# A hybrid SSD and MLP layer: first MLP product by seven quarter products, its result through DRAM, second product by token halves

## The chip, the core and the metric

The kernel runs on one core of a Trainium2 chip. The metric is device time in microseconds (us) of one execution, the median of three runs. TensorE (PE) multiplies, VectorE (DVE), ScalarE (ACT) and GpSimd (POOL) do the rest, and SyncE (SP) issues nearly all transfers, in order: a transfer that waits holds up every transfer behind it.

## The reference

One layer on 1024 tokens of 1024 channels, in float32:

```
h = x*(1+sc1) + sh1                                  # sh, sc, g: from a conditioning vector
z, xbc, dt = split(h @ w_in);  xbc = silu(conv4(xbc))
y = ssd_scan(...) + d*xs                             # Mamba-2, chunks of 64 tokens, 8 groups
y = group_rmsnorm(y * silu(z)) * norm_w              # the "gate"
x = layer_norm(alpha*x + g1 * (y @ w_out))           # w_out: 2048 x 1024
h = x*(1+sc2) + sh2
x = layer_norm(alpha*x + g2 * (relu(h @ w1)**2 @ w2))   # w1: 1024 x 4096, w2: 4096 x 1024
```

## The kernel before

Each float32 product is three TensorE passes: every operand is split into a rounded part (`...h`, a cast by `high`, line 114) and the rest (`...l`, a subtraction by `low`, line 117), and hi*hi, lo*hi and hi*lo are accumulated in PSUM. A matmul here is 128x128 weights against 128x512 columns.

**Phase A** computes `w_in` (line 141), the convolution, and the SSD group by group, in chunks (`py`, lines 357 and 362; `y`, line 366). A finished half group passes the gate: POOL multiplies by `zt` (line 385), ACT squares (388, 389), DVE adds, splits, PE sums over channels with a matrix of ones (397, 398), DVE and ACT take the inverse root (400 to 407), DVE scales (409), and SP stores it to `y_dram` (411). The last group has four such gates.

**Phase B** multiplies by `w_out` in four passes, `out_pass(T, Dh)`: token half T, output half Dh, 192 matmuls (line 584) each. Each of 16 steps loads 128 rows of `w_out` (`owr`, 557) and, for Dh=0, of `y_dram` (`yr`, 560), splits them and feeds four PSUM banks. For T=0 the split `y` tiles lie in a pool of their own (`yp0`), for T=1 partly in the second token half of `h2h`/`h2l`. At the end of a pass DVE multiplies by `g1b` (593) and adds to the row in `res`. `ln1(T)` normalises, transposes (531) and splits into `h2h`/`h2l`; `residual(T)` turns `res` into the residual of the next layer norm.

**Phase C** goes over 32 tiles of 128 FF channels. `up(f)` is 48 matmuls (653), squared ReLU and a split into `uh`/`ul`; `load2(f)` loads 128 rows of `w2`, multiplies by `g2b` (635) and splits. After every two tiles `down` adds their product, 12 matmuls (684) per 128 tokens, to `res` (690). The last four tiles are taken together, and each 128 tokens are then normalised and stored (lines 694 to 717).

The order in each engine's queue is set by a scheduler when the program is built; buffers that share memory with others wait for the last use of those. `psm` and `ps2` are the two halves of PSUM, two tiles of two banks each.

Of the kernel before, what the change touches and what calls it, by code (L numbers as in the profile page):

```python
# [9 lines left out]
F32 = mybir.dt.float32  # L10
F32R = mybir.dt.float32r
AF = mybir.ActivationFunctionType
ALU = mybir.AluOpType
# [21 lines left out]
def trunk(ctx: ExitStack, tc: tile.TileContext, a: dict, out: bass.AP):  # L35
# [5 lines left out]
    a_dram = dram.tile([NC * NH, C], F32, name="a_dram")  # L41

    # ---------------------------------------------------------------- constants
# [37 lines left out]
    mod2 = const([P, 2, KT], "mod2")          # sh2, sc2 per channel  # L81
# [76 lines left out]
    # head: conditioning, h and the first three channel tiles, k outermost  # L158
# [59 lines left out]
    def head_mm(j, w, lo):  # L218
# [8 lines left out]
        for hf in range(2):  # L227
            # the columns beside the weights are zero: each half of the tokens has its own partitions
# [31 lines left out]
    # dt, its decays and their running sums  # L260
# [152 lines left out]
    # the remaining conditioning vectors, one block of 512 columns at a time  # L413
# [69 lines left out]
    # ---------------------------------------------------------------- phase B  # L483
    ps2 = ctx.enter_context(tc.tile_pool(name="ps2", bufs=2, space=PSUM, reuse_waits="tile"))
    per = ctx.enter_context(tc.tile_pool(name="per", bufs=1, side="right", reuse_waits="tile"))
# [20 lines left out]
    lbb = lnp.tile([P, D], F32, name="lbb", tag="lbb")  # L506
    ob = ExitStack()
    ob_pool = ob.enter_context(tc.tile_pool(name="ob", bufs=2, side="right", reuse_waits="tile"))
    yp0 = ExitStack()
# [6 lines left out]


    def ln1(T, sts):
# [4 lines left out]
        for t in range(4):  # L523
            row = res[:, T * 4 + t, :]
            vec.tensor_scalar(row, row, mv[:, t, 0:1], r[:, t:t + 1], op0=ALU.subtract, op1=ALU.mult)
        ts = slice(T * 512, T * 512 + 512)
        for k in range(KT):
            if k % 2 == 0:
                pt = ps2.tile([P, 2, 512], F32, name="mm2", tag="mm2")
# [265 lines left out]
```

## Time and profile before

| | us |
|---|---|
| time, median of 3 runs | 1698.74 (1698.41 to 1700.62) |
| span of the profiled execution | 1694.5 |
| PE busy | 1603.7 (95%) |
| DVE busy | 1117.5 (66%) |
| ACT, POOL busy | 606.2 (36%), 555.4 (33%) |

The span is what the profiler saw from the first to the last instruction; no other time of that execution is given. A busy share is a mean over phases that differ: what a phase is limited by is read from the waits inside it. PEclk is the clock granted to TensorE as a share of full speed.

### The profile page before, as it was taken

To read this page: it belongs to the slowest core of one execution; us is meant where nothing else is said; L and a number is where in the kernel's file an instruction comes from. 1 tells how busy PE (TensorE), PEld (TensorE's weight loads), DVE (VectorE), ACT (ScalarE), POOL (GpSimd) and SP (SyncE) were. 2 spreads that over 40 slices of the span, in tenths; PEclk is the share of its full clock that TensorE was granted. 3 is DMA by queue.
4 is the path that set the end of the run, shared out by engine and by line. 5 is a ranking of instruction groups with operands and counts; after the bars stand their busy time and mean duration, and the time that the engine had idled before them with its cause. 6 is when DMAs were issued, how large, how long until landed. Compare 5 with 4: busy or idle time off the path is not lost.

```text
span 1694.5 us, 19835 instructions
## 1 busy us (share of the span) xinstructions
PE 1603.7 (95%) x7768; PEld 1299.6 (77%) x7768; DVE 1117.5 (66%) x1676; ACT 606.2 (36%) x720; POOL 555.4 (33%) x282
## 2 busy tenths in 40 slices
PE   6998898999999999988999889999999999999996
PEld 5886677878787777766877668888888888888884
DVE  7759988788878778877468483444444444444458
ACT  3554364555554555644342222111111111111122
POOL 2323323242424232424555442222222222222225
PEclk9999999999999999999999989999999999999998
DMA  8324433233323121134762221111111111111102
GB/s 320 123 89 137 119 100 104 96 106 106 106 94 112 63 88 63 44 120 157 231 219 73 71 66 59 50 50 50 50 49 40 48 48 42 47 42 47 38 13 99
DMA packets 56973, 151.66 MB, mean 90 GB/s; under 512 B 7344, under 2 KB 8880, under 8 KB 55984
## 3 DMA queue, kind: packets, MB, share of 16 engines
q1 hardware_dynamic: 56592, 150.37, 27.1%
q8 instruction: 61, 1.00, 0.2%
q14 instruction: 32, 0.26, 0.1%
q10 hardware_dynamic: 288, 0.03, 0.0%
HBM read 137.66 MB, written 12.71 MB: 89 GB/s over the span
## 4 chain that ended last, share of the span: by engine, by line
PE 67%; DVE 21%; issue 4%; DMA 4%; ACT 3%; POOL 1%; SPq 0%; DVEq 0%; ACTq 0%; POOLq 0%
PE mm L653 20%; PE mm L684 19%; PE mm L141 17%; PE mm L584 6%; DVE dec L344 3%; DVE mac L424 2%; DMA adr<-in_ada_r_dram 1%; DVE macc L200 1%; PE py L357 1%; PE pst L370 1%; DVE dec L347 1%; DVE Bt L154 1%; DVE y L366 1%; DVE Ct L154 1%; DVE y L117 1%
## 5 line engine op out<-in xcount | busy, mean ns | idle before, releaser
L690 DVE TENSOR_TENSOR res<-res,mm 128x1024 f32<-128x1024 f32 x119 | 145.0, 1219 | 246.5 <-PE mm L684 246.4
L141 PE MATMUL mm<-hl,whi 128*128 128x512 f32 x720 | 286.7, 398 | 0.0
L141 PE MATMUL mm<-hh,whi 128*128 128x512 f32 x720 | 286.6, 398 | 0.0
L141 PE MATMUL mm<-hh,wlo 128*128 128x512 f32 x720 | 285.8, 397 | 0.0
L653 PE MATMUL mm<-h2h,w1l 128*128 128x512 f32 x512 | 200.3, 391 | 1.6 <-POOL w1l L117 1.6
L653 PE MATMUL mm<-h2h,w1h 128*128 128x512 f32 x512 | 200.7, 392 | 1.1 <-DVE h2h L114 1.1
L653 PE MATMUL mm<-h2l,w1h 128*128 128x512 f32 x512 | 199.6, 391 | 2.2 <-POOL h2l L117 2.2
L684 PE MATMUL mm<-w2h,uh 128*128 128x512 f32 x496 | 194.3, 392 | 6.5 <-DVE res L690 6.5
L684 PE MATMUL mm<-w2l,uh 128*128 128x512 f32 x496 | 193.7, 390 | 0.0
L684 PE MATMUL mm<-w2h,ul 128*128 128x512 f32 x496 | 193.7, 390 | 0.0
L117 POOL TENSOR_TENSOR w2l<-w2r,w2h 128x1024 fp32r<-128x1024 f32 x31 | 74.4, 2419 | 347.5 <-ACT w2h L114 347.5
L117 POOL TENSOR_TENSOR wlo<-wraw,whi 128x1024 fp32r<-128x1024 f32 x45 | 111.3, 2473 | 228.8 <-ACT whi L114 228.8
L114 ACT CAST w2h<-w2r 128x1024 fp32r<-128x1024 f32 x31 | 32.6, 1052 | 352.9 <-PE mm L684 349.6
L141 PEld LDWEIGHTS mm<-hh,wlo 128*128 128x128 f32 x720 | 136.0, 189 | 28.8 <-issue 1.7
L141 PEld LDWEIGHTS mm<-hh,whi 128*128 128x128 f32 x720 | 136.0, 189 | 28.4 <-issue 1.3
L141 PEld LDWEIGHTS mm<-hl,whi 128*128 128x128 f32 x720 | 136.0, 189 | 28.3 <-issue 1.4
L351 POOL TENSOR_TENSOR ea<-ea,Ct 128x512 f32<-128x512 f32 x56 | 79.6, 1421 | 207.0 <-ACT ea L350 181.1
L584 PE MATMUL mm<-owh,y 128*128 128x512 f32 x384 | 122.7, 400 | 9.5 <-ACT y L114 4.0
L117 POOL TENSOR_TENSOR w1l<-w1r,w1h 128x1024 fp32r<-128x1024 f32 x32 | 93.9, 2936 | 111.5 <-ACT w1h L114 111.5
L117 POOL TENSOR_TENSOR owl<-owr,owh 128x512 fp32r<-128x512 f32 x61 | 90.8, 1498 | 90.4 <-ACT owh L114 86.6
L684 PEld LDWEIGHTS mm<-w2h,uh 128*128 128x128 f32 x496 | 93.5, 189 | 27.5 <-DVE res L690 8.2
L653 PEld LDWEIGHTS mm<-h2l,w1h 128*128 128x128 f32 x512 | 96.3, 188 | 23.0 <-POOL h2l L117 2.8
(239 smaller groups left out, 2974.3 us busy)
## 6 DMA issues: line engine op xcount, KB each, us to landing
wraw<-in_w_in_dram SPq DMA_DIRECT2D x45, 512.0 KB, 4.3
adr<-in_ada_r_dram SPq DMA_DIRECT2D x32, 512.0 KB, 3.5
ar<-a_dram SPq DMA_DIRECT2D x64, 256.0 KB, 3.3
owr<-in_w_out_dram SPq DMA_DIRECT2D x64, 256.0 KB, 3.1
w1r<-in_w_dram SPq DMA_DIRECT2D x32, 512.0 KB, 3.5
w2r<-in_w_dram SPq DMA_DIRECT2D x32, 512.0 KB, 3.6
y_dram<-y SPq DMA_DIRECT2D x32, 256.0 KB, 2.1
yr<-y_dram SPq DMA_DIRECT2D x32, 256.0 KB, 3.1
```

Of the source, the lines that this page charges most:

```text
L114: return (act.copy if eng is act else eng.tensor_copy)(hi, src)
L117: eng.tensor_tensor(lo, src, hi.bitcast(F32), op=ALU.subtract)
L141: pe.matmul(ps[:, hf, :], lhsT=w_[:, k, :], rhs=x_[:, k, ts], start=(k == 0 and i == 0), stop=(k == KT - 1 and i == 2))
L154: vec.scalar_tensor_tensor(dst[:, j:S], src[:, 0:S - j], convw[:, ct, 3 - j:4 - j], dst[:, j:S], op0=ALU.mult, op1=ALU.add)
L200: vec.scalar_tensor_tensor(av_, ada[:, k, :], csil[:, k:k + 1], av_, op0=ALU.mult, op1=ALU.add)
L344: vec.tensor_scalar(dec[:, h, :], ar[:, h, :], acs[:, c, g * HPG + h:g * HPG + h + 1], 0.0, op0=ALU.subtract, op1=ALU.min)
L351: pool.tensor_tensor(ea, ea, G["C"][:, ts].unsqueeze(1).broadcast_to([P, HPG, C]), op=ALU.mult)
L424: vec.scalar_tensor_tensor(acc, ad[:, i, :], csil[:, k:k + 1], acc, op0=ALU.mult, op1=ALU.add)
L584: pe.matmul(po[t // 2][:, t % 2, :], lhsT=l_[:, sl], rhs=r_, start=(k_ == 0 and i == 0), stop=(k_ == 15 and i == 2))
L653: pe.matmul(ps[:, hf, :], lhsT=w_[:, k, :], rhs=x_[:, k, ts], start=(k == 0 and i == 0), stop=(k == KT - 1 and i == 2))
L684: pe.matmul(pos[Dh], lhsT=l_[:, sl], rhs=r_[:, ds_], start=(f == fs[0] and i == 0), stop=(f == fs[-1] and i == 2))
L690: vec.tensor_tensor(row, row, po.rearrange("p a b -> p (a b)"), op=ALU.add)
```

## The change

Four things are done. (1) For FF tiles 4 to 31, taken in 14 pairs, `h @ w1` for two FF tiles and all tokens is computed by Winograd's form of Strassen's scheme: the contraction is cut into halves, FF and tokens too, and seven quarter products of 12 matmuls take the place of eight. DVE forms sums of the weight quarters (`s1` to `s4`) for each pair, and of the input blocks (`t1` to `t4`) once. Tiles 0 to 3 are computed plainly. (2) The squared ReLU is stored to `u_dram`, and the residual rows to `x1_dram`; `res` is gone, its rows live in four buffers of `rowp`. (3) The second product comes after the first is complete, by token halves `down(T)`: eight PSUM banks hold 512 tokens by 1024 channels and accumulate over all 32 tiles; `w2` and `u` are loaded and split in each half, and `g2b` is multiplied in when the banks are emptied. (4) `h2h`/`h2l` become blocks `b11`, `b12`, `b21`, `b22` in the pool on the right, and the first eight split `y` tiles use `b12` and `b22` for both token halves; the pools on the left are laid out anew.

```diff
-    h2h = per.tile([P, KT, S], F32R, name="h2h", tag="h2h")
-    h2l = per.tile([P, KT, S], F32R, name="h2l", tag="h2l")
-    res = per.tile([P, NC, D], F32, name="res", tag="res")
+    def h2_block(nm):
+        return [per.tile([P, 4, 512], F32R, name=nm + q, tag=nm + q) for q in "hl"]
+    B = {(kh, T): h2_block(f"b{kh + 1}{T + 1}") for T in range(2) for kh in range(2)}
...
+    mpa = up_.enter_context(tc.tile_pool(name="mpa", bufs=2, reuse_waits="tile"))
+    rowp = up_.enter_context(tc.tile_pool(name="rowp", bufs=4, reuse_waits="tile"))
     ob_pool = ob.enter_context(tc.tile_pool(name="ob", bufs=2, side="right", reuse_waits="tile"))
-    yp0_pool = yp0.enter_context(tc.tile_pool(name="yp0", bufs=1, reuse_waits="tile"))
+    yp = ypx.enter_context(tc.tile_pool(name="yp", bufs=1, reuse_waits="tile"))
...
-        if T == 1 and k < KT:
-            return h2h[:, k, 512:1024], h2l[:, k, 512:1024]
+        if k < KT:
+            return [b_[:, k % 4, :] for b_ in B[k // 4, 1]]
...
+    def product(dst, w, x, first=False):
+        for k in range(4):
+            for i, (w_, x_) in enumerate(((w[0], x[0]), (w[1], x[0]), (w[0], x[1]))):
+                pe.matmul(dst, lhsT=w_[:, k, :], rhs=x_[:, k, :], start=(first and k == 0 and i == 0),
+                          stop=(k == 3 and i == 2), skip_group_check=not first)
...
+    def up_quad(p):
+        r0, r1 = load1(f0), load1(f1)
...
+        vec.tensor_tensor(s[2], a11, a21, op=ALU.subtract)
+        vec.tensor_tensor(s[0], a21, a22, op=ALU.add)
+        vec.tensor_tensor(s[1], s[0], a11, op=ALU.subtract)
+        vec.tensor_tensor(s[3], a12, s[1], op=ALU.subtract)
+        a1 = forms1(r0)
...
+        product(X, [w_[:, 0:4, :] for w_ in a1], X11, True)
+        product(Q, F["s3"], TF["t3"], True)
+        act.copy(Y, X)
+        product(Y, F["s2"], TF["t2"])
+        act.copy(q7, Q)
+        product(X, [w_[:, 4:8, :] for w_ in a1], X21)
+        act.copy(Z, Y)
+        act.activation(u0[:, 0:512], X, AF.Relu)
+        product(Y, F["s1"], TF["t1"])
+        vec.tensor_tensor(u1[:, 512:S], Y, q7, op=ALU.add)
+        product(Z, F["a22"], TF["t4"])
+        vec.tensor_tensor(u1[:, 0:512], Z, q7, op=ALU.add)
+        product(Y, F["s4"], X22)
+        vec.scalar_tensor_tensor(u1, u1, 0.0, u1, op0=ALU.max, op1=ALU.mult)
+        u_store(f1, u1)
+        act.activation(u0[:, 512:S], Y, AF.Relu)
+        pool.tensor_tensor(u0, u0, u0, op=ALU.mult)
+        u_store(f0, u0)
...
+    def load2(f, T):
         sp.dma_start(w2r, a["w2"][f])
+        sp.dma_start(ur, u_dram[f][:, T * 512:T * 512 + 512])
...
+        split(ur, uh, ul, act, vec)
+        split(w2r, w2h, w2l, act, vec if f % 2 == 0 else pool)
...
+    def down(T):
+        po = [(psm.tile([P, 2, 512], F32, name="mm", tag="mm") if t < 2 else
+               ps2.tile([P, 2, 512], F32, name="mm2", tag="mm2")) for t in range(4)]
...
+        KF = 4
+        for f in range(NF - KF):
+            ops = load2(f, T)
+            for t in range(4):
+                for Dh in range(2):
+                    mms(f, t, Dh, ops)
...
+            sp.dma_start(row, x1_dram[tt])
...
+                vec.tensor_tensor(tm[:, q], src[:, q], g2b[:, q], op=ALU.mult)
+                vec.tensor_tensor(row[:, q], row[:, q], tm[:, q], op=ALU.add)
```

How the queues change is shown at three places. First SP at the end of phase A, before; `y_dram12` and `y_dram13` are the stores of the first of the last four gates.

```order
L325 DMA ar_6279<-a_dram_73 128x512 [waits DMAHW3_49,DVE_49]
L557 DMA owr_6449<-in_w_out_dram 128x512 [waits DMAHW6_49,Pool_49]
L560 DMA yr_6451<-y_dram0_57 128x512 [waits DMAHW7_49]
L557 DMA owr_6474<-in_w_out_dram 128x512
L560 DMA yr_6476<-y_dram1_58 128x512
L557 DMA owr_6498<-in_w_out_dram 128x512
L557 DMA owr_6522<-in_w_out_dram 128x512 [waits DMAHW6_49,DVE_49]
L560 DMA yr_6500<-y_dram2_59 128x512 [waits DMAHW7_49,DMAHW4_49,DVE_49]
```

The same place in the changed kernel; `DMAHW...` is a wait for earlier transfers, here the four last stores of `y_dram`.

```order
L413 DMA y_dram12_69<-y_5147 128x512 [waits DVE_49]
L413 DMA y_dram13_70<-y_5147 128x512 [waits DMAHW4_49,DVE_49]
L413 DMA y_dram12_69<-y_5423 128x512 [waits DMAHW5_49,DVE_49]
L413 DMA y_dram13_70<-y_5423 128x512 [waits DVE_49]
L413 DMA y_dram14_71<-y_5812 128x512 [waits DVE_49]
L413 DMA y_dram15_72<-y_5812 128x512 [waits DMAHW0_49,DVE_49]
L413 DMA y_dram14_71<-y_6082 128x512 [waits DMAHW1_49,DVE_49]
L413 DMA y_dram15_72<-y_6082 128x512 [waits DMAHW2_49,DVE_49]
L571 DMA owr_6500<-in_w_out_dram 128x512 [waits DMAHW3_49,DMAHW4_49,DMAHW2_49,DMAHW1_49]
L574 DMA yr_6502<-y_dram0_57 128x512 [waits DMAHW7_49,DMAHW0_49]
```

The first loads of phase B stood ahead of the last gates' stores; now they stand behind all of them, and the first of them waits for the last stores, since its buffer takes over memory of the last gates.

Second, PE at the same time, before: the matrix of ones (`pr`) of a gate among the matmuls of the first pass.

```order
L584 MATMUL mm_6447<-owh_6647,y0_8_6650 128x512
L398 MATMUL pr_6375<-sl_6372,ones_r_91 128x512
L584 MATMUL mm_6447<-owl_6648,y0_8_6650 128x512
L584 MATMUL mm_6447<-owh_6647,y1_8_6651 128x512
L584 MATMUL mm_6447<-owh_6647,y0_8_6650 128x512
```

PE in the changed kernel, where the last gate's two `pr` matmuls and the first matmul of the first pass stand.

```order
L359 MATMUL py_6339<-dec_6329,X_6325 64x128 x2
L364 MATMUL py_6339<-ea_6336,hn_6260 64x128 x2
L359 MATMUL py_6339<-dec_6329,X_6325 64x128 x2
L364 MATMUL py_6339<-ea_6336,hn_6260 64x128 x2
L399 MATMUL pr_6442<-sh_6438,ones_r_131 128x512
L400 MATMUL pr_6442<-sl_6439,ones_r_131 128x512
L598 MATMUL mm_6498<-owh_6504,b12h_6474 128x512
L598 MATMUL mm_6499<-owh_6504,b12h_6474 128x512
```

No matmul of the first pass stands ahead of the last gate's any more.

Third, SP towards the end of phase C, before: weights of both products in turn.

```order
L612 DMA w1r_11660<-in_w1_dram 128x1024
L612 DMA w1r_11729<-in_w1_dram 128x1024
L634 DMA w2r_11666<-in_w2_dram 128x1024
L634 DMA w2r_11735<-in_w2_dram 128x1024
L612 DMA w1r_11798<-in_w1_dram 128x1024
L634 DMA w2r_11804<-in_w2_dram 128x1024
```

SP in the changed kernel, from the last pair of FF tiles to the second product; `xrow` are the residual rows.

```order
L665 DMA u_dram31_105<-row_10247 128x1024
L803 DMA xrow_11417<-x1_dram0_106 128x1024
L803 DMA xrow_11467<-x1_dram1_107 128x1024
L803 DMA xrow_11515<-x1_dram2_108 128x1024
L803 DMA xrow_11565<-x1_dram3_109 128x1024
L803 DMA xrow_12673<-x1_dram4_110 128x1024
L665 DMA u_dram30_104<-row_10246 128x1024
L771 DMA w2r_10361<-in_w2_dram 128x1024
L773 DMA ur_10363<-u_dram0_74 128x512
```

The first load of `w2` now stands behind the last store of the first product and behind five loads of residual rows, the second of which waits for the last matmuls of the first product.

## Rows read from the trace of the kernel before

**Rows 1.** The page's first part: busy time, share of the span, instructions of each engine.
```profile
PE 1603.7 (95%) x7768; PEld 1299.6 (77%) x7768; DVE 1117.5 (66%) x1676; ACT 606.2 (36%) x720; POOL 555.4 (33%) x282
```

**Rows 2.** Windows: stretch, length, busy time by engine, PEclk, DMA share, GB/s.
```profile
741.00:807.00 66.00, 54.04 (x245) 41.14 (x244) 49.74 (x71) 31.63 (x51) 28.18 (x17) 0.92 0.49 156
807.00:958.00 151.00, 144.45 (x634) 117.63 (x633) 85.18 (x104) 45.75 (x75) 80.26 (x53) 0.98 0.49 161
958.00:1012.00 54.00, 39.15 (x162) 29.46 (x161) 47.23 (x51) 16.63 (x25) 27.18 (x12) 0.87 0.15 49
1108.00:1632.00 524.00, 524.00 (x2313) 434.04 (x2312) 243.03 (x165) 97.66 (x96) 127.59 (x48) 1.00 0.14 45
```

**Rows 3.** Chain that ended last, towards the end: start, us, what.
```profile
1602.94 5.44 PE mm L684 x24
1608.38 23.80 PE mm L653 x105
1632.18 9.99 PE mm L684 x44
...
1680.36 4.46 PE mm L684 x12
1684.83 0.69 DVE res L687
```

**Rows 4.** Timeline of PE around the start of phase B: start, us, instruction, idle before.
```profile
741.50 0.40 PE L398 MATMUL pr<-sl,ones_r 128*128 128x512 f32 x1
745.23 1.19 PE L584 MATMUL mm<-owh,y 128*128 128x512 f32 x2 [3.34 <-ACT r L403]
...
800.45 0.80 PE L584 MATMUL mm<-owh,y 128*128 128x512 f32 x1 [3.96 <-ACT y L114]
801.04 0.63 PE L584 MATMUL mm<-owl,y 128*128 128x512 f32 x1
...
806.89 0.85 PE L584 MATMUL mm<-owh,y 128*128 128x512 f32 x3
```

**Rows 5.** Timeline of DVE: last step of two gates, and the first pass's end.
```profile
751.50 2.44 DVE L409 SCALAR_TENSOR_TENSOR y<-y,nwcol,r 128x512 f32<-128x512 f32 x2
...
805.64 1.42 DVE L409 SCALAR_TENSOR_TENSOR y<-y,nwcol,r 128x512 f32<-128x512 f32 x2
807.32 1.29 DVE L593 TENSOR_TENSOR tm<-mm,g1b 128x512 f32<-128x512 f32 x2 [0.26 <-PE mm L584]
```

**Rows 6.** Groups by line, 741 to 808 us: busy us, mean ns, idle before.
```profile
L385 POOL TENSOR_TENSOR y<-y,zt 128x1024 f32<-128x1024 f32 x2 | 4.7, 2370 | 9.9 <-ACT zt L444 6.9 <-DVE y L366 3.0
```

**Rows 7.** DMA issues: count, KB each, median us to landing.
```profile
owr<-in_w_out_dram SPq DMA_DIRECT2D x64, 256.0 KB, 3.1
w2r<-in_w_dram SPq DMA_DIRECT2D x32, 512.0 KB, 3.6
y_dram<-y SPq DMA_DIRECT2D x32, 256.0 KB, 2.1
```

**Rows 8.** What PE waited for from 740 us: us in total, times, longest.
```profile
PE mm L531 <- DVE res L525: 12.4, 3, 7.4
PE mm L684 <- DVE res L690: 6.5, 4, 4.6
```

**Rows 9.** Windows: the second pass of the output product.
```profile
815.00:855.00 40.00, 39.83 (x177) 32.65 (x176) 16.57 (x25) 13.10 (x23) 20.28 (x15) 1.00 0.74 245
```

**Rows 10.** Groups by line, 1100 to 1632 us: steady phase C.
```profile
L117 POOL TENSOR_TENSOR w1l<-w1r,w1h 128x1024 fp32r<-128x1024 f32 x24 | 70.8, 2952 | 85.6 <-ACT w1h L114 85.6
L114 ACT CAST w2h<-w2r 128x1024 fp32r<-128x1024 f32 x24 | 25.3, 1053 | 314.0 <-PE mm L684 314.0
```

**Rows 11.** Timeline of DVE in the last stage: evictions and normalisation.
```profile
1671.46 1.22 DVE L690 TENSOR_TENSOR res<-res,mm 128x1024 f32<-128x1024 f32 x1
...
1676.31 2.29 DVE L498 TENSOR_TENSOR rq<-rr 128x1 f32<-128x1 f32 x1
...
1679.09 1.22 DVE L690 TENSOR_TENSOR res<-res,mm 128x1024 f32<-128x1024 f32 x1
```

More of the change, by code (lines that the diff above doesn't have):

```diff
@@ L668, in down @@
-    def down(fs, toks, final=False):
-        for t in toks:
-            sl = slice(t * P, (t + 1) * P)
-            po = ps2.tile([P, 2, 512], F32, name="mm2", tag="mm2")
-            last = final and t == NC - 1
-            pos = [po[:, 0, :], (ps2.tile([P, 2, 512], F32, name="mm2", tag="mm2") if last else po)[:, 1, :]]
-            row = res[:, t, :]
-            steps = [(f, Dh) for f in fs for Dh in range(2)]
+    yt, sts = [], []
+    out_pass(1, 0, yt, sts)
+    ws1 = [forms1(load1(f)) for f in range(2)]
@@ new lines, in trunk, with up_plain @@
+    out_pass(1, 1, yt, sts)
+    ob.close()
+    ypx.close()
+    NS = 4
+    lt1 = ExitStack()
+    lt = lt1.enter_context(tc.tile_pool(name="lt", bufs=2, reuse_waits="tile"))
+    tst = ExitStack()
+    tpool = tst.enter_context(tc.tile_pool(name="tpool", bufs=1, side="right", reuse_waits="tile"))
+    h2q = {}
+    ups = {}
+    def up_plain(f, w, T):
+        if T == 0:
+            pl_, tg = (psm, "mm") if f % 4 < 2 else (ps2, "mm2")
+            ups[f] = pl_.tile([P, 2, 512], F32, name=tg, tag=tg)
+        for k in range(KT):
+            bh, bl = B[k // 4, T]
+            for i, (w_, x_) in enumerate(((w[0], bh), (w[1], bh), (w[0], bl))):
+                pe.matmul(ups[f][:, T, :], lhsT=w_[:, k, :], rhs=x_[:, k % 4, :],
+                          start=(k == 0 and i == 0), stop=(k == KT - 1 and i == 2))
@@ new lines, in u_store, with up_evict @@
+    def u_store(f, u, cols=slice(0, S)):
+        sp.dma_start(u_dram[f][:, cols], u[:, cols])
+    def up_evict(f):
+        u = rowp.tile([P, S], F32, name="row", tag="row")
+        act.activation(u, ups[f].rearrange("p a b -> p (a b)"), AF.Relu)
+        vec.tensor_tensor(u, u, u, op=ALU.mult)
+        u_store(f, u)
+    up_plain(0, ws1[0], 0)
+    up_plain(1, ws1[1], 0)
+    ln1(1, sts, lt, h2q)
+    up_plain(0, ws1[0], 1)
+    up_plain(1, ws1[1], 1)
+    residual(1)
+    ws2 = [forms1(load1(f)) for f in range(2, NS)]
@@ new lines, in trunk @@
+    for kk in range(4):
+        t4 = lt.tile([P, 512], F32, name="t1f", tag="t1f", bufs=4)
+        vec.tensor_tensor(t4, B[1, 0][0][:, kk, :].bitcast(F32), h2q[1, kk], op=ALU.subtract)
+        vec.tensor_tensor(t4, t4, B[1, 0][1][:, kk, :].bitcast(F32), op=ALU.add)
+        split(t4, TF["t4"][0][:, kk, :], TF["t4"][1][:, kk, :], act, vec)
+    for f in range(2, NS):
+        up_evict(f)
+    lt1.close()
+    mp = up_.enter_context(tc.tile_pool(name="mp", bufs=1, reuse_waits="tile"))
+    X11, X21, X22 = B[0, 0], B[1, 0], B[1, 1]
@@ L737, in trunk @@
-    down((0, 1), hi4)
-    for f in range(3, NF):
-        up(f, load(f), both)
-        if f % 2 == 0 and f < NF - 2:
-            down((f - 2, f - 1), range(NC))
-    down((NF - 4, NF - 3, NF - 2, NF - 1), range(NC), final=True)
+                mms(NF - KF + f, t, Dh, ops[f])
+            parts = [slice(0, 512), slice(512, D)] if last else [slice(0, D)]
+            for i, q in enumerate(parts):
+                tm = dr.tile([P, D], F32, name="tm2", tag="tm2", bufs=2)
+                src = po[t].rearrange("p a b -> p (a b)")
+                vec.tensor_tensor(tm[:, q], src[:, q], g2b[:, q], op=ALU.mult)
+                vec.tensor_tensor(row[:, q], row[:, q], tm[:, q], op=ALU.add)
@@ L745 @@
+    down(0)
+    down(1)
 def kernel(**inputs):
```

247 lines of the change are left out of this document (122 added, 125 removed).

## The prediction, made before the result was known

> **What bounds the kernel now.** The page's first part comes first: PE is busy for 95% of the span, DVE for 66%, ACT and POOL for a third [rows 1]. So I looked for what PE has to do and where it does nothing, by the windows and the chain. In steady phase C PE is busy all of the 524 us at full clock [rows 2], and the chain's rows give the price of a matmul there: 24 in 5.44 us, 0.2267 us each [rows 3]. Phase C has 3072 of them, 696 us: fewer matmuls there shorten the span one for one. PE loses time at three places. At the start of phase B it has 12 idle us of 66 [rows 2], though the matmuls of the first output pass already run between the last gates of phase A: the last matrix of ones of an early gate is at 741.50, the first pass starts at 745.23 and its result is taken at 807.32 [rows 4, 5]. Around the second layer norm (958 to 1012 us) PE is busy for 39 of 54 us at a clock of 0.87 [rows 2]; the transposes wait 12.4 us in all for normalised rows [rows 8]. And at the end: the last 192 matmuls begin at 1632.18 and would take 43.5 us, but the span ends at 1694.5, 18.8 us beyond that; PE waits there for DVE, once 4.6 us, to empty a bank [rows 3, 8].
>
> **What is saved.** 14 pairs of FF tiles need 84 in place of 96 matmuls for each half: eight quarter products of 12 become seven, so 12 fewer a pair, 168 in all: 168 x 0.2267 = 38.1 us. Forms and copies cost nothing if they hide behind the 84 x 0.2267 = 19.0 us of a pair. POOL has the low part of one FF tile (2.95 us), a square of 1024 columns as at line 385 (2.37) and half a low part (1.5), 6.8 us [rows 6, 10]. ACT has a cast of 1.05 us [rows 10], five of half that size and five copies and ReLUs of 512 columns, at 0.6 us each: 7. DVE has some twelve steps of 0.69 us, like the one of 512 columns at 1684.83 [rows 3], 8 us, and some lengthening beside POOL. In the program's order each copy inside the seven products has at least one other product (12 matmuls, 2.7 us) between it and its reader. So I take nothing, and count uncovered copies as a rival.
>
> The second product keeps its 1536 matmuls. Its loads double: 0.52 MB of w2 and 0.26 MB of u for each 5.44 us are 145 GB/s, where the second output pass took 245 at a DMA share of 0.74 without harm to PE [rows 9]. The splits, 1.7 us of ACT and at most 2.4 of POOL or 1.9 of DVE a tile, fit into 5.44. Nothing.
>
> **The start of phase B.** This is the largest term against the change. The loads of the first pass now stand on SP behind the stores of all four last gates, and wait for them; on PE no matmul of the pass stands ahead of the last gate's. PE therefore idles where it now works. When is the last gate stored? The first gate has all its inputs at 741.9 as before and is scaled by about 753 [rows 4, 5]. DVE takes its work in order, so the second follows after its root (ACT, then DVE, 6 us) and the chunks' steps queued there, about 763; the last chunk's output comes at about 767. The last gate is then a chain of its own: POOL 2.37 [rows 6], two squares, a sum and a split (2.3), the matrix of ones twice with a step between (1.8), DVE, a table load, three of ACT and three of DVE (6), 1.42 for the scaling [rows 5]: 14 us, and some 2 us of hops. Five 512 KB loads of w1, with their casts on ACT and POOL, are put among it. Done at about 783. Then a store of 2.1 us and a load of 3.1 [rows 7], a cast: PE starts at about 788. The pass has 192 matmuls, 43.5 us, and begins with a cold PE: before, after an idle 3.96 us, the 16 matmuls recorded from 800.45 to 806.89 took 6.4 us and not 3.6 [rows 4], 2.8 lost. With 2 us for its loads it ends at 836 in place of 807.3: **29 us lost**. Bounds: with no waits among the gates PE starts at 778 and 17 are lost; at the pace of the four gates before, whose last ended at 807 [rows 5], it starts past 800 and 41 are lost. I take the middle, nearest to the chain.
>
> **The rest of phase B and the second layer norm.** From 807 to 958 PE was busy for 144 of 151 us [rows 2]. The passes are the same; the residual rows are stored in addition and the row loads wait for these stores: +1 (0 to 5). From 958 to 1012: 145 of the 3072 matmuls were done by 1012 (from there to 1632.18 there is room for 2735, and 192 follow), 32.9 us of 54, so 21 were lost. After it, DVE has no w2 to multiply there, but forms t1 to t4; and PE has only tiles 0 to 3, and no second product, to fill the wait for rows. I put 24: +3 (-7 to +13). The first pair waits for four evictions, t4 and its own forms on DVE; four or five steps of 0.69 us [rows 3] stand uncovered: +3 (1 to 6).
>
> **From the first product to the second.** Before, both were interleaved and nothing waited. Now the first w2 stands on SP behind the last u store. After the last matmul: ReLU 0.6, square on POOL 2.4, store issued at +3.1. Ahead of it stand five 512 KB loads of rows; four of them wait for nearly the last matmul. These 2.1 MB, the store, the first w2 and u are 3.4 MB; at 245 / 0.74 = 331 GB/s [rows 9] 10.3 us, and 1.3 us of latency (a 256 KB store takes 2.1 [rows 7], of which 0.8 is its bytes). With a cast the first matmul comes at +12.2, then 2.8 for the cold clock: **15 us lost**. If the row loads cost nothing: 3.1 + 3.6 [rows 7] + 1.05 [rows 10] + 1.4, 9; with queueing behind all of them 20. From the first token half to the second: the last bank is emptied behind another tile's evictions, +1 (0 to 4).
>
> **The end.** DVE needed 7.6 us for 128 tokens (first steps at 1671.46 and 1679.09), a small step of it stretched to 2.29 us beside POOL [rows 11]. Now each has a multiply of 1.2 us more, while PE delivers one every 5.44. But only four token tiles are left in the last stage, and each has banks of its own, so PE doesn't wait. POOL works beside two of the four; with 8.5 us for these and 6 for the others, an estimate, DVE has 29 us of work, starts 16.3 us before PE's end, ends 12.7 after it, and the last store takes 3: 16 against 18.8 before: -2.8 (-8 to +1).
>
> **Sum.** -38.1 + 29 + 1 + 3 + 3 + 15 + 1 - 2.8 = +11.1 us. On the profiled span, 1694.5, that gives 1705.6; the median lies 4.2 above that span, in which I change nothing: 1709.8, 0.65% slower. I take 1710.
>
> **Rivals.** *The gates overlap better (faster).* Place: phase A's end. The four gates are independent but for the engines; if they run side by side, the last one's chain starts with its last chunk, which needs no gate before it. With that chunk done at 750 and 16 us for the chain, the store and load put PE's start at 772 and the pass's end at 820: 13 lost in place of 29, and 1694. It decides from a start at 777, where the change breaks even. For it: only 12 of 66 us of PE were idle while everything was interleaved. Against: DVE had 50 of 66 us busy there [rows 2], of which the pass's own splits move behind the gates, and w1's casts come in. Chance 0.24, with a lighter hand-over to the second product among it.
>
> *About no change.* Half of that gain (8), or the light hand-over (6), not both: 1702 to 1704, and with a little more, 1700. The same rows speak for and against it. Chance 0.14.
>
> *The seven products aren't covered.* Two copies late by 1 us in each pair: 14 x 2 = 28 us, 1738. For it: each form has one buffer, and DVE steps lengthen beside POOL [rows 11]. Against: 5 us of cover by the order for most. Chance 0.08.
>
> *The second product loses clock.* PE now goes through eight banks in turn, three matmuls each. With the clock of 0.87 of the window 958 to 1012 [rows 2] its 348 us would grow by 52: 1762. Against it: the output pass goes through four banks in the same way, and had PE at 1.00 and busy for 39.83 of 40 us [rows 9]. Chance 0.02. The Trainium skill (TensorE: Matmul & The Clock Gate, "A second HAM failure mode: psum-queue depth-cycling") says that cycling through PSUM banks each iteration can let PE idle briefly so often that its clock swings. By that rule the second product would slow; the four-bank pass in this trace doesn't agree, so I leave it this small.
>
> The likeliest keeps 0.52. Changes under 0.2%, 3.4 us, can't be told from none: faster 0.24, same 0.14, slower 0.62. The range of the bounds around the likeliest is 1696 to 1732; with the rivals I give 1691 to 1734.
>
> **What would show it.** The first matmul of the output product at 780 to 795 us and PE idle before it; about 19.0 us for 84 matmuls of a pair without gaps; PE idle for 10 to 14 us between the two products, then slow matmuls; no wait for DVE by PE at the end, but 14 to 18 us after its last matmul. I am wrong if the first pass starts before 777, if pairs take over 20 us, or if the layer norm's window grows by more than 13 us.

## The result, and the profile after

The changed kernel took 1721.7 us (median of 4 runs, 1717.4 to 1727.58) against 1698.8 before: a ratio of 1.0125, with an interval of 1.0097 to 1.0153. It is 22.9 us slower. The forecast was 1710 (slower by 11). So its sign and its range held, and half of the loss was missing from it. In a second comparison the ratio was 1.0121 (1.01 to 1.0142).

The profiled execution took 1727.58 us, its span is 1725.8. The page's first part answers to [rows 1]: 168 matmuls are gone, and DVE is busy for less time than before.

```profile
PE 1581.5 (92%) x7600; PEld 1278.6 (74%) x7600; DVE 1097.7 (64%) x1765; ACT 683.7 (40%) x892; POOL 570.0 (33%) x300
```

PE is busy for 22 us less and the span is 31 us longer, so look for where PE stands still. The windows answer to [rows 2] (stretch, length, busy time by engine, PEclk, DMA share, GB/s):

```profile
748.00:797.00 49.00, 11.41 (x61) 6.99 (x59) 29.76 (x49) 18.70 (x26) 11.12 (x5) 0.54 0.35 116
797.00:844.00 47.00, 45.72 (x185) 36.48 (x186) 15.58 (x24) 15.66 (x27) 18.64 (x14) 0.94 0.70 232
844.00:988.00 144.00, 142.00 (x640) 116.62 (x639) 84.68 (x104) 43.62 (x73) 73.25 (x51) 1.00 0.45 144
988.00:1071.00 83.00, 60.46 (x216) 44.99 (x214) 64.28 (x79) 24.52 (x38) 38.84 (x16) 0.75 0.20 70
1071.00:1343.00 272.00, 265.69 (x1162) 219.08 (x1162) 142.17 (x153) 86.88 (x148) 79.61 (x40) 0.99 0.29 102
1343.00:1360.00 17.00, 2.98 (x9) 2.15 (x8) 2.50 (x3) 4.18 (x6) 3.04 (x2) 0.58 0.98 352
1360.00:1543.00 183.00, 182.11 (x798) 150.29 (x796) 70.26 (x80) 56.72 (x75) 49.41 (x21) 0.99 0.46 148
1543.00:1709.00 166.00, 165.78 (x731) 137.28 (x732) 69.70 (x81) 48.27 (x66) 50.75 (x20) 1.00 0.45 148
1709.00:1725.00 16.00, 0.68 (x4) 0.22 (x2) 13.44 (x29) 1.85 (x5) 3.50 (x2) 0.66 0.33 131
```

Three stretches stand out: the first (last gates, PE almost idle), the fourth (second layer norm and the way into the seven products, PE busy at a clock of 0.75) and the sixth (from the first product to the second). The seven-product pairs (1071 to 1343) and the second product (from 1360) run at a granted clock of 0.99 to 1.00. What PE waited for from 740 us, answering to [rows 8] (us in total, times, longest):

```profile
PE mm L789 <- ACT uh L116: 14.0, 1, 14.0
PE mm L598 <- DVE b12h L116: 12.8, 1, 12.8
PE mm L661 <- DVE b12l L119: 9.2, 2, 8.0
...
PE mm L714 <- DVE s3l L119: 4.7, 1, 4.7
PE mm L661 <- POOL b22l L119: 3.3, 1, 3.3
...
PE mm L661 <- DVE b12h L116: 2.9, 2, 1.5
```

L598 is the output product, L661 a plain FF tile, L714 the seven products, L789 the second MLP product. The chain shows the first and the last of the three places, in order of time:

```profile
789.07 0.75 DVE y L411
...
789.84 2.01 DMA y_dram<-y
...
792.34 4.02 DMA yr<-y_dram
...
1343.29 0.61 ACT row L754
...
1343.96 1.90 POOL row L755
...
1345.88 0.32 SPq L665
...
1347.21 10.01 DMA w2r<-in_w_dram
...
1357.27 17.79 PE mm L789 x66
```

The last gate's store and its load back stand between the gates and the output product, whose first matmul PE's timeline has at 796.96:

```profile
796.96 1.19 PE L598 MATMUL mm<-owh,b12h 128*128 128x512 f32 x2 [12.83 <-DVE b12h L116]
```

Between the products stand a ReLU, POOL's square, the store on SP, and a w2 load of 10 us in a window whose DMA share is 0.98.

An account of the time needs the same marks in each kernel: the last projection matmul of phase A, DVE's eviction that ends the first output pass, DVE's first eviction of the last output pass, the end of the span. DVE's timeline of the changed kernel has the second and the third, answering to [rows 5]:

```profile
843.98 1.29 DVE L608 TENSOR_TENSOR tm<-mm,g1b 128x512 f32<-128x512 f32 x2 [7.51 <-PE mm L598]
...
987.48 1.28 DVE L610 SCALAR_TENSOR_TENSOR row<-row,mm 128x512 f32<-128x512 f32 x2 [11.19 <-PE mm L598]
```

The times between the marks, from one profiled execution of each kernel in this text (medians are those of its runs):

| kernel | median us | phase A | to end of first pass | rest of phase B | from there to the end |
|---|---|---|---|---|---|
| before | 1698.8 | 741.0 | 66.3 | 151.2 | 736.0 |
| changed | 1721.7 | 748.0 | 96.0 | 143.5 | 738.3 |
| changed again | 1720.8 | 742.6 | 95.7 | 143.3 | 739.0 |
| overlap | 1709.7 | 741.9 | 67.5 | 165.8 | 729.4 |
| forms later | 1709.4 | 739.3 | 96.4 | 142.3 | 729.1 |
| quick hand-over | 1720.1 | 743.9 | 96.2 | 143.8 | 734.6 |
| all three | 1696.1 | 742.9 | 66.8 | 163.9 | 721.1 |
| overlap, stores later | 1702.2 | 745.0 | 66.3 | 163.9 | 725.6 |
| plain first product | 1732.4 | 745.2 | 96.0 | 142.4 | 746.8 |
| entry order | 1706.3 | 743.8 | 96.0 | 142.3 | 722.5 |
| all three, entry order | 1690.5 | 745.9 | 67.5 | 164.4 | 712.8 |
| the same, six plain tiles | 1678.3 | 742.0 | 66.3 | 165.8 | 699.6 |
| the same, no seven products | 1705.5 | 744.7 | 66.7 | 163.2 | 728.7 |

Phase A scatters from 739 to 746 us between profiles, 748 in the first of the changed kernel, with the same order of its matmuls in the changed kernel and before; I take this for scatter, though an effect of the change of a few us can't be excluded. The rest: +29.7, -7.7, +2.3 us in the first profile, +29.4, -7.9, +3.0 in the second. The last column is the surprise: 168 matmuls are gone there, 38 us, and it isn't shorter.

In that column, from 987.48 (first eviction of the last pass) to the first matmul of the second product at 1357.27 are 369.8 us. The matmuls in it, 4 tiles of 48 and 14 pairs of 84, are 1368, 310.1 us at 0.2267 [rows 3]. Lost are 59.7: 14.0 at the hand-over and 45.7 around the second layer norm and the entry to the pairs. There DVE is the engine to read. Its timeline in the middle of the layer norm (start, us, instruction):

```profile
1021.56 4.62 DVE L553 TENSOR_TENSOR row<-row,lg 128x1024 f32<-128x1024 f32 x4
...
1027.03 0.68 DVE L119 TENSOR_TENSOR b12l<-h,b12h 128x512 fp32r<-128x512 f32 x1
...
1030.05 4.62 DVE L554 TENSOR_TENSOR row<-row,lbb 128x1024 f32<-128x1024 f32 x4
...
1063.06 1.23 DVE L670 TENSOR_TENSOR row<-row 128x1024 f32<-128x1024 f32 x1 [13.57 <-ACT row L669]
```

And POOL's in the same place:

```profile
1027.19 10.40 POOL L119 TENSOR_TENSOR b22l<-h,b22h 128x512 fp32r<-128x512 f32 x1 [6.11 <-DVE b22h L116]
1037.56 1.29 POOL L119 TENSOR_TENSOR t1l<-t1f,t1h 128x512 fp32r<-128x512 f32 x1
```

And PE, which waits for both:

```profile
1027.77 0.79 PE L661 MATMUL mm<-b12l,w1h 128*128 128x512 f32 x1 [7.96 <-DVE b12l L119]
...
1037.65 0.50 PE L661 MATMUL mm<-b22l,w1h 128*128 128x512 f32 x1 [3.26 <-POOL b22l L119]
```

The residual of the token half just normalised (L553, L554) and steps of t1 to t4 stand on DVE ahead of the last split that PE needs, 0.68 us of work. Then POOL's split of 1.3 us takes 10.4 beside DVE's unbroken row of steps. So PE comes late to its last plain tiles, 2 and 3 (from 1041 us), and now DVE stands still, 13.57 us, for the eviction of one of them (L669, L670); t4, which DVE splits from 1065 on into the memory of b12, and the first pair's forms come only after that. The two engines wait for each other in turn.

### The profile page after: what moved, and what is told of

The parts are those of the page before. It is cut to its first block, busy times and chain, and to the rows that moved or that the text cites. A ratio compares the mean times of both kernels' runs of the same rounds, so it can differ in the third digit from the quotient of the medians.

```text
span 1725.8 us, 20338 instructions
## 1 busy us (share of the span) xinstructions
PE 1581.5 (92%) x7600; PEld 1278.6 (74%) x7600; DVE 1097.7 (64%) x1765; ACT 683.7 (40%) x892; POOL 570.0 (33%) x300
## 4 chain that ended last, share of the span: by engine, by line
PE 62%; DVE 21%; DMA 6%; issue 5%; ACT 3%; POOL 3%; SPq 0%; DVEq 0%; POOLq 0%; ACTq 0%
PE mm L789 19%; PE mm L143 16%; PE mm L714 15%; PE mm L598 5%; DVE dec L346 3%; DVE mac L426 2%; DMA adr<-in_ada_r_dram 2%; PE mm L661 2%; DMA yr<-y_dram 1%; POOL owl L119 1%; DVE macc L202 1%; PE pst L372 1%; DVE dec L349 1%; DVE xd L343 1%; PE py L359 1%
## 5 line engine op out<-in xcount | busy, mean ns | idle before, releaser
L789 PE MATMUL mm<-w2h,uh 128*128 128x512 f32 x512 | 199.2, 392 | 15.1 <-ACT uh L116 14.0
L789 PE MATMUL mm<-w2l,uh 128*128 128x512 f32 x512 | 199.8, 391 | 0.0
L789 PE MATMUL mm<-w2h,ul 128*128 128x512 f32 x512 | 199.1, 390 | 0.0
L119 DVE TENSOR_TENSOR ul<-ur,uh 128x512 fp32r<-128x512 f32 x64 | 58.8, 923 | 186.9 <-ACT uh L116 186.9
L143 PEld LDWEIGHTS mm<-hh,wlo 128*128 128x128 f32 x720 | 137.0, 190 | 29.4 <-issue 1.7
L789 PEld LDWEIGHTS mm<-w2h,uh 128*128 128x128 f32 x512 | 96.7, 189 | 36.1 <-ACT uh L116 14.4
L116 ACT CAST uh<-ur 128x512 fp32r<-128x512 f32 x64 | 39.8, 622 | 191.8 <-PE mm L789 187.0
L789 PEld LDWEIGHTS mm<-w2l,uh 128*128 128x128 f32 x512 | 96.8, 189 | 20.2
L789 PEld LDWEIGHTS mm<-w2h,ul 128*128 128x128 f32 x512 | 96.5, 189 | 20.1
L346 DVE TENSOR_SCALAR dec<-ar,acs 128x128 f32<-128x128 f32 x256 | 101.3, 450 | 7.3 <-PE py L359 7.3
L348 ACT ACTIVATE dec<-dec 128x512 f32<-128x512 f32 x64 | 40.1, 627 | 122.3 <-DVE dec L346 109.4
L598 PE MATMUL mm<-owh,y 128*128 128x512 f32 x256 | 80.4, 391 | 0.0
L116 ACT CAST w2h<-w2r 128x1024 fp32r<-128x1024 f32 x64 | 67.0, 1046 | 20.1 <-DMA w2r<-in_w_dram 19.6
```

Source lines behind the costliest of these rows:

```text
L116: return (act.copy if eng is act else eng.tensor_copy)(hi, src)
L119: eng.tensor_tensor(lo, src, hi.bitcast(F32), op=ALU.subtract)
L143: pe.matmul(ps[:, hf, :], lhsT=w_[:, k, :], rhs=x_[:, k, ts], start=(k == 0 and i == 0), stop=(k == KT - 1 and i == 2))
L346: vec.tensor_scalar(dec[:, h, :], ar[:, h, :], acs[:, c, g * HPG + h:g * HPG + h + 1], 0.0, op0=ALU.subtract, op1=ALU.min)
L348: act.activation(dec, dec, AF.Exp)
L598: pe.matmul(po[t // 2][:, t % 2, :], lhsT=l_[:, sl], rhs=r_, start=(k_ == 0 and i == 0), stop=(k_ == 15 and i == 2))
```

## The experiments

**The changed kernel again**, beside three that change one thing each.

> The changed kernel itself, unaltered, for a second trace and times beside the others. Theory: what the first trace shows belongs to the kernel, so the output product starts 48 to 49 us after phase A's last projection matmul, the two products are 14 us apart, and the time lies at 1717 to 1728 us. Phase A's end at 748 us instead of 742 I take for scatter of that one execution: it should end at 740 to 749 here. Rival: phase A itself is slower in the changed kernel; then it ends at 748 or later again.

Measured: 1720.75 us (1717.33 to 1722.65). The output product starts 48.3 us after phase A, the products are 14.1 apart, and phase A ends at 742.6: the theory held, and the rival did not. Its profile gives the third row of the table; it is the base of what follows.

**The overlap put back at the start of phase B.** The y tiles of the first token half get a pool of their own, so that the first pass's loads stand among the last gates again:

```
+    yps = [ypx.enter_context(tc.tile_pool(name="yp0", bufs=1, ...))]
-        if k < KT:
+        if T == 1 and k < KT:
...
+    ypx.close()
+    mpa = up_.enter_context(tc.tile_pool(name="mpa", bufs=2, ...))
...
+    yps.append(ypx.enter_context(tc.tile_pool(name="yp", bufs=1, ...)))
```

> Only memory moves: the first 16 split y tiles of token half 0 get a pool of their own on the left, the residual rows go to the right, and a gap puts the output product's buffers where they were in the kernel before. The loads of the first pass again stand ahead of the last gates' stores. Theory (the first pass was held up by its buffers alone): first output matmul at 745 to 752 us, first pass ends about 29 us earlier than in the changed kernel, time 1686 to 1698. Rival (the gates are what takes the time, and the pass would wait for DVE and ACT anyway, since w1's casts now run there): pass ends after 825, time 1705 to 1720.

Measured: 1709.73, ratio to before 1.006 (1.004 to 1.008). The first output matmul is at 746.2 and the first pass ends 67.5 us after phase A in place of 95.7: the 28 us of the theory are there. But the theory's time, 1686 to 1698, was missed. The time is in the rival's range, though not for the rival's reason, a pass that ends after 825 (it ends at 809): the rest of phase B takes 165.8 instead of 143.3, and 22 of the 28 go back. PE's waits in pass (1,0), 852 to 927 us:

```profile
PE mm L601 <- DVE y L119: 6.5, 2, 6.2
PE mm L601 <- ACT y L116: 5.6, 2, 4.3
```

The last column is 9.6 shorter; the hand-over had 5.2 us of idle time here instead of 14.1, with another memory layout.

**The overlap with the x1 stores later.** One suspect was SP: the stores of x1, which wait for DVE's residual, stood ahead of the y loads of pass (1,0). They are issued behind its last weight load here, and the rows have a pool of their own:

```
-    residual(0)
...
     out_pass(1, 0, yt, sts)
+    with tc.issue_after(queue["w"]):
+        residual(0)
```

> The overlap of the first output pass with the last gates, as before, but the x1 stores of T=0 (with the residual that makes them) issued behind the last loads of pass (1,0) and rows in a pool of their own. In the run with the overlap alone, pass (1,0) took 73.5 us against 57, and PE waited there for y. Theory: its y loads stood on SP behind those stores, which wait for the residual. With the stores out of the way pass (1,0) takes 57 to 60 us and the time is 1692 to 1697, a further 13 to 17 below that run's 1709.7. Rival: the loads themselves are late (rows, y and wo in the same two passes, while DVE and ACT split them): then pass (1,0) stays over 68 us and the time at 1705 to 1712.

Measured: 1702.23, ratio 1.0019 (1.0004 to 1.0034). The theory was wrong: the rest of phase B is still 163.9, pass (1,0) 71.5, over the rival's 68. The time lies below the rival's 1705, and the last column, which the theory did not speak of, is 3.8 shorter than with the overlap alone. SP now waits for y's splits, 834 to 926 us (the first row) and DVE has a busy share of 0.9 just then (the second, a window):

```profile
SPq L576 <- DVE y L119: 20.3, 6, 16.2
```

```profile
854.00:874.00 20.00, 16.11 (x69) 12.68 (x68) 18.11 (x25) 5.93 (x10) 13.45 (x8) 0.94 0.81 273
```

The first layer norm and y's splits meet on DVE, near to what the rival said. In the changed kernel ACT casts y of the second half from 848 to 892, nearly all of it during pass (0,1), tile by tile as that pass's matmuls free the buffers; here the last eight tiles are cast only from 895 on, inside pass (1,0). With that goes the changed kernel's gain of 8 us over before in this column. Whether DVE alone decides, or also that y's second half takes over memory of the first, was not separated.

**Forms later.** The residual of the second half and the steps of t1 to t4 are issued behind the last splits of b12 and b22, and the last low part of b22 goes from POOL to DVE:

```
-    residual(1)
+    with tc.issue_after(queue["lo"]), tc.issue_after(queue["h2"]):
+        residual(1)
```

> Only the order on DVE at the second layer norm changes: the residual multiplications and the block forms t1 to t4 are issued behind the last split of b12 and b22, and the last low part of b22 is made by DVE. Theory (PE waits there for splits that stand behind 1024-column residual steps): the waits of line 661's matmuls for b12l and b22l, 12.5 us in the trace of the changed kernel, fall to under 3, the time by 8 to 12 us, to 1709 to 1714. Rival (DVE is the bound of this stretch, 52 of 56 us busy): the work only moves, the first pair waits for t forms by as much more, time within 3 us of the changed kernel.

Measured: 1709.43 (1708.68 to 1715.57), ratio 1.0069 (1.0042 to 1.0095): the 11 us of the theory, and the last column is 9.9 shorter. The wait for b12l is gone. In its place PE waits once for 11.6 us, for the low part of a w1 tile on POOL. That row of POOL, beside an unbroken row of DVE steps:

```profile
1006.60 15.33 POOL L119 TENSOR_TENSOR w1l<-w1r,w1h 128x1024 fp32r<-128x1024 f32 x2 [7.71 <-ACT w1h L116]
```

**Quick hand-over.** The last pair's square goes to ACT, its store to ACT's queue, and the x1 rows are loaded behind the ninth w2 load:

```
+            act.activation(u0, u0, AF.Square)
+            act.dma_start(u_dram[f0], u0)
...
+            load_behind(row, x1_dram[tt], "w2")
```

> Only the hand-over between the two products changes: the last pair's square and store are issued by ACT, so that SP isn't held up, and the residual rows are loaded behind the ninth w2. Theory (PE waits for w2 and u because of their place on SP): the gap between the last product of the first and the first matmul of the second shrinks from 14.0 to 3 to 5 us and the time by 10 to 12, to 1709 to 1712. Rival (the transfers are the limit, DMA share 0.98 in these us): a gap of 9 us or more, gain under 5.

Measured: 1720.05 (1719.22 to 1721.3); the last column is 4.4 shorter. The wait fell from 14.1 to 5.05 us, but PE stood again a little later, for a low part of w2 on DVE. PE's timeline:

```profile
1344.91 2.07 PE L795 MATMUL mm<-w2h,uh 128*128 128x512 f32 x4 [5.05 <-ACT uh L116]
...
1351.15 2.07 PE L795 MATMUL mm<-w2l,uh 128*128 128x512 f32 x4 [4.17 <-DVE w2l L119]
```

Half of the gain became a new wait. The gap fell nearly as the theory had it (3 to 5 us), but neither its time, 1709 to 1712, nor a clear gain came of it: the runs of the two kernels overlap. The rival's gap of 9 us or more did not come, though its gain of under 5 did. So most of the 14 us came from the order on SP and from POOL's square, which the edit changes together.

**Plain first product.** The seven products undone alone: 28 more plain tiles, no t forms; the rest of the change kept.

```
-    for p in range(NS // 2, NF // 2):
-        up_quad(p)
+    for f in range(NS, NF):
+        w = forms1(load1(f))
+        for T in range(2):
+            up_plain(f, w, T)
+        up_evict(f)
```

> The changed kernel with the first MLP product plain: 96 matmuls for each pair and half, eight quarter products in place of seven, the rest of the change kept (result through DRAM, second product by token halves, phase B's order). Theory: 168 matmuls more at 0.2267 us, all on the path: 38 us over the changed kernel, 1759 (1755 to 1762), PE without waits in the pairs in both. Rival, that forms and copies of the seven products cost PE something per pair: then the plain product costs less than 38 more, by 1 us a pair 24: 1745.

Measured: 1732.38 (1731.02 to 1733.07), 11.6 over the changed kernel, where the theory had 38 and the rival 24. This is the run that shows where the expected gain went. Its windows:

```profile
984.00:1024.00 40.00, 30.77 (x119) 22.65 (x118) 30.87 (x43) 10.13 (x14) 15.21 (x6) 0.85 0.29 105
1024.00:1344.00 320.00, 320.00 (x1410) 264.96 (x1409) 35.70 (x30) 56.04 (x57) 69.90 (x28) 1.00 0.25 92
1344.00:1362.00 18.00, 4.89 (x23) 3.73 (x21) 1.80 (x2) 2.59 (x3) 0.00 (x0) 0.76 0.74 269
```

From the last pass to the second product are 378.4 us here, for 1536 matmuls (348.2): 30.2 lost, against 59.7 and 60.5 in the two profiles of the changed kernel. The hand-over costs about the same in both (PE waits 13.1 and 14.0). So the pairs' steady part saves its 38 us, and the entry to them, not each pair as the rival had it, takes back some 29: while DVE forms t1 to t4, PE has only plain tiles 0 to 3 to do.

**All three edits**, with the stores later:

> All four edits on the changed kernel: token tile 0's y tiles and rows in memory of their own, so that the first output pass may run among the last gates; the x1 stores of T=0 issued behind the last loads of pass (1,0); the residual of T=1 and the t forms behind the last splits of b12 and b22; and the quick hand-over. Theory that the three places (start of phase B, second layer norm, hand-over) are separate losses which add: from 1720.8, about 28 at the start, 11 at the layer norm and 3 at the hand-over come back, 42 in all: 1679, that is 20 us (1.2%) below the kernel before. Rival, that what is gained at the start is given back in the passes that follow, as 17 of the 28 were with the overlap alone, whatever the place of the x1 stores: 1720.8 - 11 - 11 - 3 = 1696, no change against the kernel before.

Measured: 1696.14, ratio 0.9987 (0.9975 to 0.9998). That is what the rival gave, level with before, and 17 above the theory. The rest of phase B is 163.9, so the start's gain is given back as with the overlap alone, and the last column is 17.9 shorter than in the changed kernel.

**The entry's order.** Is the entry's price one of order, which engine splits what and when, or of work on DVE? Low parts of three w1 tiles (plain tiles 2 and 3, and the first pair's) go from POOL to DVE, the two plain ones ahead of half of the residual; tiles 2 and 3 take the second token half first, so that t4 may start earlier; the first pair's cast stands before t4's. First on the kernel with the forms later, then on the one with all three:

```
+        residual(1, 0)
+    ws2 = [forms1(load1(f), vec) for f in range(2, NS)]
+    with tc.issue_after(queue["w1l"]):
+        residual(1, 1)
...
+    for f in range(2, NS):
+        for T in (1, 0):
+            up_plain(f, ws2[f - 2], T)
```

> The changed kernel with the order around the second layer norm alone altered: as in the run with the forms later (residual and t forms behind the last splits of b12 and b22), and further the low parts of the w1 tiles 2 and 3 and of the first pair on DVE instead of POOL, the former ahead of half of the residual's steps; tiles 2 and 3 take the second token half first, so that b12 comes free for t4 earlier; the first pair's cast ahead of t4's. In the plain run the way from the last output pass to the end of the first product lost about 30 us, in the changed kernel about 60 (both with the 14 of the hand-over), so the entry to the seven products costs some 30 us over the plain one. Theory: that price is only one of order, since PE waits there for low parts that POOL makes in 10 us each beside dense DVE work: PE's wait of 11 us for w1l goes and the first pair starts 15 to 20 us earlier than in the run with the forms later (1709.4): 1690 to 1695. Rival: the price is work, DVE has some 40 us of steps between the last split and the first pair's forms and PE's four plain tiles cover only part of it, in whatever order: the wait moves to the first pair and the time stays above 1702.

> The combined kernel (1696.1 on its runs: overlap, stores later, forms later, hand-over) with the same further edits around the second layer norm. Theory (order): 15 to 20 us less, 1676 to 1681, below the kernel before by over 1%. Rival (work): not below 1690.

Measured: 1706.28 (ratio 1.004, 1.0025 to 1.0056) and 1690.53 (0.9953, 0.9936 to 0.9969). The theory's 1690 to 1695 and 1676 to 1681 were missed; the rivals named 1702 and 1690, and both times lie above. PE's wait for w1l before tile 2 went from 11.6 to 1.3 us and from 11.4 to 1.2, but the wait moved to the first pairs. In the second of these kernels PE has, from 965 us on:

```profile
PE mm L735 <- POOL w1l L119: 6.6, 1, 6.6
PE mm L735 <- ACT w1h L116: 6.5, 1, 6.5
```

Both waits are for the second pair's first weights: the scheduler put that product of 12 matmuls ahead of the first pair's other products, whose s3l DVE finishes only at 1051:

```profile
1049.24 1.76 DVE L119 TENSOR_TENSOR s3l<-s,s3h 128x512 fp32r<-128x512 f32 x1
```

The windows show why: DVE works without a gap while PE has run out of plain tiles.

```profile
1025.00:1035.00 10.00, 9.90 (x44) 7.72 (x42) 10.00 (x6) 1.02 (x2) 10.00 (x7) 1.00 0.01 2
1035.00:1045.00 10.00, 0.80 (x1) 0.29 (x1) 10.00 (x14) 4.68 (x8) 5.61 (x2) 0.73 0.19 78
1045.00:1055.00 10.00, 6.18 (x18) 4.92 (x19) 7.30 (x8) 2.94 (x6) 5.46 (x2) 0.58 0.38 119
```

So this order is worth 3 and 6 us in the medians, and the larger part of what is left is work on DVE: from the last split at 1000.1 to s3l at 1051.0 it is busy for 49.7 of 50.9 us, PE for 35. Some of that work is lengthening (steps of 0.68 us take 1.7 and more beside POOL), which these runs do not price apart.

**Six plain tiles.** If so, PE needs more plain work beside the forms: six plain tiles and 13 pairs instead of four and 14.

```
-    NS = 4
+    NS = 6
...
+        if f >= 4:
+            ws2.append(forms1(load1(f), vec))
```

The low parts of the two further tiles are made by DVE as well.

> The combined kernel with the altered entry order, and six FF tiles plain ahead of the seven-product pairs instead of four (13 pairs instead of 14). That run showed DVE busy without a gap from 995 to 1051 while PE had only the plain tiles 2 and 3 and one quarter product to do, and stood for some 19 us before the first pair's other products. Theory (the entry's price is work on DVE, and PE needs plain tiles to cover it): two more plain tiles give PE 21.8 us beside it and cost 12 matmuls more, 2.7 us; the idle 15 to 19 us go: 1674 to 1679. Rival (the chain of forms grows with it, because t4 waits until the last plain tile has read b12, and the pair's own forms stand behind t4 on DVE): the idle time moves behind the new tiles and the time is 1688 to 1694.

Measured: 1678.27 (1675.41 to 1679.39), ratio 0.9884 (0.9865 to 0.9904): within the theory's range, 43 us below the changed kernel, and faster than the kernel before by 1.2%. It does 12 matmuls more than the kernel above and is 12.3 us faster. DVE is as busy at the entry as in the kernel above (50.2 of 52 us from 1000 on), but now PE is busy for 49.4 of them. Two windows, the entry and the pairs:

```profile
1010.00:1040.00 30.00, 30.00 (x134) 24.54 (x133) 28.81 (x30) 11.58 (x17) 23.42 (x8) 1.00 0.43 164
1040.00:1300.00 260.00, 258.43 (x1138) 213.00 (x1136) 135.93 (x151) 87.72 (x148) 75.02 (x37) 1.00 0.30 105
```

**The same without seven products**, to price the pairs where their forms are covered:

> The kernel with six plain tiles (1678.3, where PE waits nowhere in the first product) with a plain first product throughout: no seven-product pairs and no t forms. It measures what 13 pairs of seven products are worth where their forms are covered. Theory: all of the matmuls saved, 13 x 12 = 156 at 0.2267 us, 35.4 us: 1713 to 1715. Rival: the forms and copies, or the entry, still cost something there, so that the plain product is slower by 25 us or less: at most 1703.

Measured: 1705.47 (1700.05 to 1713.46), ratio 1.0047 (1.0025 to 1.0068): 27.2 above in the medians, 29.1 in the last column, where the theory had 35.4 and the rival at most 25. The runs of this kernel scatter by 13 us, so that its median can't be told from the rival's 25, and the last column is one profile of each. Of the 6 us between 35.4 and 29.1, some are in rows. In the layer norm the granted clock of the kernel with pairs falls where the other's stays at 1.00; the same window, first with pairs, then without:

```profile
1004.00:1010.00 6.00, 4.80 (x15) 3.86 (x15) 6.00 (x7) 1.24 (x2) 5.19 (x1) 0.72 0.56 149
```

```profile
1004.00:1010.00 6.00, 6.00 (x28) 4.96 (x28) 5.52 (x5) 0.00 (x0) 0.00 (x0) 1.00 0.75 258
```

That one window does 13 fewer recorded matmuls, about 3 us; the last pair's two waits (0.9 and 0.7) and a hand-over longer by 1.2 (5.4 against 4.2) are the rest, nearly. So 13 covered pairs are worth 27 to 29 us by these runs, not 35.

The entry's loss can now be set side by side: the time from the first eviction of the last output pass to the first matmul of the second product, less its matmuls at 0.2267 us and the hand-over's wait. It is 45.7 and 46.3 us in the changed kernel, 36.0 with the forms later, 29.6 with the entry's order, 29.2 with all three edits and the entry's order, and 13.1 with six plain tiles. With a plain first product it is 17.1 in the changed kernel's order and 7.5 in the altered one. The price of the seven products at the entry is thus 29 us in the first order, 22 in the second, and 6 with six plain tiles.

## Why the prediction was right, and where it was not

- **The saving.** Right. 14 pairs of 84 matmuls took 272 us with 265.7 of PE busy, 19.4 a pair, as against 19.0 forecast; the only waits in them are 4.7 at the very start and 1.6 in the last pair. The rival of uncovered pairs is out.
- **The start of phase B.** Right: predicted 29 lost, measured 29.7 and 29.4, and 28.2 came back when the overlap was put back alone. The steps hold one by one: the last gate stored at about 790, phase A having ended 7 us late in that profile (forecast 783), and the output product started 49 us after phase A (forecast 47). Nothing of the faster rival, which needed a start before 777, is seen.
- **The rest of phase B.** Wrong in sign: +1 was forecast, -7.7 measured. The step counted stores and rows added, and overlooked where y's second half is split: in the changed kernel from 848 to 892, nearly all before pass (1,0), while before the change the last eight tiles were cast from 853 to 881, inside that pass. In the overlap runs, where they are cast inside it again, the column is over 20 us longer than in the changed kernel. What of this the late start gives and what the new place of the y tiles was not separated.
- **The second layer norm and the first pair.** This is the step that failed, in its size. I took 24 lost and 3 for the first pair, 27, and the far ends of both bounds gave 40. The profiles have 45.7 and 46.3. The text said that I was wrong if this window grew by more than 13 us: even without the first pair's 4.7 it grew from 21 to 41. The working counted four or five DVE steps as uncovered. It did not look at what stands on DVE ahead of the last splits (PE waits 8.0 and 3.3 us for two of them in the changed kernel), and it did not add up DVE's steps up to the first pair: residual, t forms, evictions, the pair's own forms. With these splits put first, as in the kernel with all three edits and the entry's order, DVE's row behind them takes 51 us, 49.7 of them busy, while PE has 96 plain matmuls, 22 us. By the losses side by side the seven products cost 29 us at the entry; issuing the forms later took 10 from the loss, the entry's order 6 more, two more plain tiles 16.
- **From the first product to the second.** Right: predicted 12.2 idle, 2.8 for the clock and 1 for the change of halves, 16 in all; measured 14.0, and 4.2 lost in the 1536 matmuls that follow, 18.
- **The second product, and the end.** Right: the granted clock stays at 0.99 and 1.00 through eight banks in turn, at 148 GB/s (145 forecast); the end is 16.1 us behind the last matmul (1709.7), as forecast. The Trainium skill (TensorE: Matmul & The Clock Gate, "A second HAM failure mode: psum-queue depth-cycling") tells of a kernel whose clock swings as it cycles through the banks; the second product here, at 0.99 and 1.00, does not show it, and that rival is out.

So the two errors, 19 us too little at the entry and 9 too much in the rest of phase B, partly cancelled, and that was luck. What they leave, 10 us, is most of the 12 by which the time lies above the forecast. Without the second error the time would have been near 1730, still within the range of 1691 to 1734. But that range was not added up from the bounds of the steps, which together reach from 1673 to 1751, and the entry lay beyond its own bounds: that the range held says little about that step.

## What to carry to other kernels

A transformation that saves matmuls needs forms first. Before counting its saving, add up the busy time of the engine that makes them, from its first input to the first use, and set it against the work that the matmul engine has meanwhile; if it is short, leave some of the plain work there, since each plain pair here cost 2.7 us and covered 21.8. And put the splits that the next matmul reads ahead of everything that may come later on the same queue.

## What the runs showed of the hardware

A POOL step that takes 1.3 us (512 columns) or 2.5 (1024) elsewhere was held in three places while DVE issued steps with two inputs from SBUF without a break: 10.40 us for one of 512 columns in the changed kernel, 15.33 for two of 1024 with the forms later, 17.34 for two of 512 in the kernel with all three edits and the entry's order:

```profile
1008.50 17.34 POOL L119 TENSOR_TENSOR t1l<-t1f,t1h 128x512 fp32r<-128x512 f32 x2 [9.94 <-ACT t1h L116]
```

In each of the three, POOL's first step ended only once a gap had opened in DVE's row. But a dense row does not always hold POOL: behind that gap, in the same kernel, POOL's and DVE's steps go side by side for some 12 us, and now DVE's of 512 columns are longer too, 1.7 to 1.8 us in place of 0.68:

```profile
1028.01 1.78 DVE L119 TENSOR_TENSOR t2l<-h,t2h 128x512 fp32r<-128x512 f32 x1
```

```profile
1029.19 1.73 POOL L119 TENSOR_TENSOR t1l<-t1f,t1h 128x512 fp32r<-128x512 f32 x1
```

The Trainium skill (SBUF — State Buffer, "Who interferes with whom") says that a DVE instruction with two SBUF inputs contends with a GpSimd instruction that reads SBUF, and that the order of issue decides who blocks. The rows agree that the two contend, and add that the wait can last far longer than one DVE step. What decides between the two patterns was not tested. Spans on POOL are rough, but PE's wait for the result bears the 15.33 out: 11.6 us in the kernel with the forms later.
